# Attention's reciprocal sums go through the maxima's transpose and DRAM instead of four transposes a pair of heads

## The chip, the cores and the metric

The kernel runs on one core of a Trainium2 chip. The metric is the device time of one execution in microseconds (us); 2429.42 us is the median of three runs before the change (2428.42 to 2429.88). The engines named here are PE (TensorE, with PEld for its weight loads), DVE (VectorE), ACT (ScalarE), POOL (GpSimd) and SP, whose queue issues nearly all DMAs. Each engine works through its own queue in order.

## What is computed

The reference is one trunk layer over 2048 positions of 1024 channels: an RMS norm, one projection `W_in`, a spatial-gating group A, an attention group B, `W_out`, then a convolutional FFN and a last norm. The change lies in group B, eight heads of 64 channels:

```python
s = einsum('bhtd,bshd->bhts', qi, k) * scale
s = s + ci[..., :, None] - c[:, :, None, :]      # c: cumulated log-sigmoid of the forget logits
s = where(kpos[None, :] <= qpos[:, None], s, -inf)
p = softmax(s, axis=-1)
return einsum('bhts,bshd->bthd', p, v)
```

The softmax needs for each query the maximum of its scores and the sum of the exponentials; the output of a head is divided by that sum.

## The kernel before

All matmuls of the projections run with operands split into a high and a low float32r part (`mm3`, lines 208 to 212: three matmuls for one product). Phase A computes the projections of two halves of the sequence, phase C the output projection, phase D the FFN's up-projection, and a last phase the down-projection.

Attention is a stream (`b_stream`) of 32 pieces: four blocks of 512 queries (tb = 0 to 3), and in each eight heads. It is a Python generator that the big matmul loops advance: `tick` counts their matmuls, and for every 3.5 to 4.4 of them (`RATES`) the stream makes one step, so that its instructions are laid between those of the projections. A `yield` ends a step. The instructions so traced are then ordered, engine by engine, by a planner that gives each instruction a priority by its place in the program and times it with its own cost figures; the order in each queue is fixed at compile time.

A head has two parts:

- `b_max(h, tb)` loads the queries (`t1`, `t2`) and keys, computes the scores with queries on partitions (lines 750 and 751), takes their minima on DVE (754, 756; the sign is turned), exponentials with sums on ACT (759), and at its end the maxima `m8` (767, 768) and, by way of `lw` and `l1`, the reciprocal `rr` of the sum (773 to 778, for the first block 780): four numbers for each of 128 partitions, for the 4 x 128 queries.
- `b_mix(h, tb, ...)` computes the scores again with keys on partitions (811, 812), with the maxima as rows 96 to 104 of the stationary query tile `t1`, then the exponentials (817), their split (822, 823) and the product with the values into `po` (799, 800).

Between them stands `turn`: PE transposes `m8` (128x8, line 784) into a bank of the score ring, and DVE multiplies it by a selection mask `rowsel` into `t1` (785). The order of the work is `b_max(h+1)`, then `b_mix(h)`, which runs the `turn` of head h+1 at its step `TURN` = 3, then `b_max(h+2)`.

At the end of `b_mix` the two heads of a pair have written the halves of the partitions of `op` (834, 835). After the odd head the reciprocals of both heads are needed along the free axis, the same for 64 partitions of a head: ACT widens `rr` to `rw`, 128x512 (840); after a step, `transpose4` makes four PE transposes of 128x128 (line 183) into one bank of the score ring; and DVE multiplies `op` by it from PSUM (843). The result is split (196, 197) and stored to `mixh` and `mixl` in DRAM, from where the output projection reads it.

The score ring has three PSUM banks, with two more of another pool in the later part (`scores`). `op` and `rw` have one buffer each.

Of the kernel before, what the change touches and what calls it, by code (L numbers as in the profile page):

```python
# [80 lines left out]
class Block:  # L81
# [134 lines left out]
    def constants(self):  # L216
        nc, a, tc = self.nc, self.a, self.tc
        cp = self.cpool = self.ctx.enter_context(tc.tile_pool(name="const", bufs=1))
        self.ident = cp.tile([P, P], F32, name="ident")
        make_identity(nc, self.ident)  # L220
        self.mhalf = cp.tile([P, 8], F32, name="mhalf")
        nc.gpsimd.memset(self.mhalf, -0.5)
        self.cols = cp.tile([P, 200], F32, name="cols")
        self.halo = cp.tile([P, 2 * NF, 2], F32, name="halo")
        nc.gpsimd.memset(self.halo, 0.0)
        dp = self.ctx.enter_context(tc.tile_pool(name="dram", bufs=1, space=DRAM))
        self.ones_d = dp.tile([2, HALF], F32, name="ones_d")
        t = lambda n, k, s: [dp.tile(s, F32, name=f"{n}{i}") for i in range(k)]
        self.qx = t("qx", 2, [8, 128, HALF])
        self.kx = t("kx", 2, [8, 132, HALF])  # L230
        self.cc = t("cc", 2, [8, 2, HALF])
        self.vd = t("vd", 2, [HALF, 8, P])
        self.mixh = t("mixh", 4, [D, TB])
        self.mixl = t("mixl", 4, [D, TB])
        self.rows_d = [t(f"rows{i}_", 8, [P, D]) for i in range(2)]
        self.act_d = [t(f"act{i}_", NF, [P, HALF]) for i in range(2)]
        self.tw_d = t("tw", NF // 2, [P, 2, D])

    def columns(self):

# [409 lines left out]
    def b_consts(self):  # L650
        nc, bp = self.nc, self.bp
        ones = self.til(self.sp, [P, TB], F32, "st")[:2, :]
        nc.gpsimd.memset(ones, 1.0)
        for i in range(2):
            self.dma(self.ones_d[:, i * TB:(i + 1) * TB], ones)
        for k in self.kx:
            self.dma(k[:, 128:130, :], self.ones_d.unsqueeze(0).broadcast_to([8, 2, HALF]))
        self.mask = bp.tile([P, TB], BF16, name="mask")
        nc.gpsimd.memset(self.mask, 0.0)

        nc.gpsimd.affine_select(out=self.mask, in_=self.mask, compare_op=ALU.is_ge, fill=BIG, base=384,
                                pattern=[[-1, TB]], channel_multiplier=1)

        self.maskT = bp.tile([P, P], BF16, name="maskT")
        nc.gpsimd.memset(self.maskT, 0.0)
        nc.gpsimd.affine_select(out=self.maskT, in_=self.maskT, compare_op=ALU.is_ge, fill=BIG, base=0,
                                pattern=[[1, P]], channel_multiplier=-1)

        self.rowsel = bp.tile([8, 4, P], BF16, name="rowsel")
        nc.gpsimd.memset(self.rowsel, 1.0)  # L670
        for base, mult in ((0, 1), (1, -1)):
            nc.gpsimd.affine_select(out=self.rowsel, in_=self.rowsel, compare_op=ALU.is_ge, fill=0.0, base=base,
                                    pattern=[[-2 * mult, 4], [0, P]], channel_multiplier=mult)
        self.M1, self.T1 = [[self.til(self.mp, [P, TB], F32R, tag) for _ in range(2)] for tag in ("m1", "t1")]
        for m in self.M1:
            nc.gpsimd.memset(f32(m[64:128, :]), 0.0)
            nc.gpsimd.memset(f32(m[96:104, :]), 1.0)
        for t in self.T1:
            nc.gpsimd.memset(f32(t[64:128, :]), 0.0)
            self.dma(f32(t[66:68, :]), self.ones_d[:, 0:TB])  # L680

    def b_stream(self, pieces):

        todo = None
        for h, tb in pieces:
            if tb >= 2 and not self.ready:
                if todo:
                    yield from self.b_mix(*todo, None)
                    self.done += 1
                    todo = None  # L690
                while not self.ready:
                    yield
            t1, t2, turn = yield from self.b_max(h, tb)
            if todo:
                yield from self.b_mix(*todo, turn)
                self.done += 1
            else:
                turn()
            todo = (h, tb, t1, t2, self.rr)
        yield from self.b_mix(*todo, None)  # L700
        self.done += 1

# [27 lines left out]
    def b_max(self, h, tb):  # L730
# [8 lines left out]
        self.dma(f32(t2), self.qx[hf][h, :, sl])  # L739
        nm = self.til(bp, [P, 4, 4], F32, "part")  # L740
        ls = self.til(bp, [P, 4, 4], F32, "ls")
        if h % 2 == 0:
            self.rr = self.til(bp, [P, 4, 2], F32, "rr")
        for sb in range(tb + 1):
            m1, m2 = self.b_keys(h, sb, False)
            for tt in range(4):
# [16 lines left out]
            nc.vector.tensor_reduce(mx, nm[:, :, 0:tb + 1], axis=AX.X, op=ALU.min)  # L763
        else:
            nc.vector.tensor_copy(mx, nm[:, :, 0])
        m8 = self.til(bp, [P, 4, 2], F32R, "m8")
        nc.vector.tensor_scalar(m8[:, :, 0], mx, -1.0, None, ALU.mult)
        nc.vector.scalar_tensor_tensor(m8[:, :, 1], mx, -1.0, f32(m8[:, :, 0]), op0=ALU.mult, op1=ALU.subtract)
        rr = self.rr[:, :, h % 2]
        if tb:  # L770
            k = slice(0, tb + 1)
            lw = self.til(bp, [P, 4, 4], F32, "lw")
# [7 lines left out]
            nc.vector.reciprocal(rr, ls[:, :, 0])  # L780

        def turn():
            pm = self.scores([8, P])
            nc.tensor.transpose(pm, f32(m8).rearrange("p a b -> p (a b)"), self.ident)
            nc.vector.tensor_tensor(t1[96:104, :].rearrange("p (a b) -> p a b", a=4),
                                    pm.unsqueeze(1).broadcast_to([8, 4, P]), self.rowsel, op=ALU.mult)

        return t1, t2, turn

    def b_mix(self, h, tb, t1, t2, rr, turn):  # L790

        nc, bp, pp = self.nc, self.bp, self.bpp
        po = self.til(pp, [P, TB], F32, "o")
        ns = 4 * tb + 4
        late = []

        def pv():
            sc, c, v, ph, pl = late.pop(0)
            nc.tensor.matmul(po[:, c], lhsT=v, rhs=ph[:, c], start=sc == 0, stop=False)  # L799
            nc.tensor.matmul(po[:, c], lhsT=v, rhs=pl[:, c], start=False, stop=sc == ns - 1)  # L800

        for sc in range(ns):
            if sc == TURN and turn:
                turn()
            if sc % 4 == 0:
                m1, m2, v4 = self.b_keys(h, sc // 4, True)
            j = max(0, sc - 4 * tb)
            c = slice(j * P, TB)
            ks = slice((sc % 4) * P, (sc % 4 + 1) * P)
            ps = self.scores([P, TB])  # L810
            nc.tensor.matmul(ps[:, c], lhsT=m1[:, ks], rhs=t1[:, c], start=True, stop=False)  # L811
            nc.tensor.matmul(ps[:, c], lhsT=m2[:, ks], rhs=t2[:, c], start=False, stop=True)  # L812
            if sc >= 4 * tb:
                d = ps[:, j * P:(j + 1) * P]
                nc.vector.tensor_tensor(d, d, self.maskT, op=ALU.add)  # L815
            e = self.room([P, TB], F32, "e")
            nc.scalar.activation(e[:, c], ps[:, c], AF.Exp, scale=-1.0)  # L817
            if len(late) >= (LAG + 1 if self.more else LAG):
                pv()
            ph = self.room([P, TB], F32R, "ph")  # L820
            pl = self.room([P, TB], F32R, "pl")
            nc.scalar.activation(ph[:, c], e[:, c], AF.Copy)  # L822
            nc.vector.tensor_tensor(pl[:, c], e[:, c], f32(ph[:, c]), op=ALU.subtract)  # L823
            late.append((sc, c, v4[:, sc % 4, :], ph, pl))
            yield
        while late:
            pv()
            yield

        if h % 2 == 0:  # L830
            self.op = self.til(self.mp, [P, TB], F32, "op")
        op = self.op
        own, other = (slice(0, 64), slice(64, 128)) if h % 2 == 0 else (slice(64, 128), slice(0, 64))
        nc.scalar.activation(op[own, :], po[other, :], AF.Copy)
        nc.vector.tensor_tensor(op[own, :], po[own, :], op[own, :], op=ALU.add)
        if h % 2 == 0:
            return

        rw = self.til(self.mp, [P, 4, 2, 64], F32, "rw")
        nc.scalar.activation(rw, rr.unsqueeze(3).broadcast_to([P, 4, 2, 64]), AF.Copy)  # L840
        yield
        pr = self.transpose4(None, "s", [rw[:, i, :, :].rearrange("p a b -> p (a b)") for i in range(4)])
        nc.vector.tensor_tensor(op, pr, op, op=ALU.mult)
        oh = self.room([P, TB], F32R, "ph")
        ol = self.room([P, TB], F32R, "pl")
        self.split_sb(op, oh, ol)
        cs = slice(512 + (h - 1) * 64, 512 + (h + 1) * 64)
        self.dma(self.mixh[tb][cs, :], f32(oh))
        self.dma(self.mixl[tb][cs, :], f32(ol))
# [666 lines left out]
```

## Time and profile before

| | |
|---|---|
| median of the runs | 2429.42 us (2428.42 to 2429.88) |
| profiled execution | 2425.31 us, of which the span from first to last instruction 2423.6 us |
| granted TensorE clock, mean | 0.999 |
| PE / DVE / ACT / POOL busy | 2404.0 / 1755.0 / 1352.4 / 315.8 us |
| DMA | 400.51 MB, mean 165 GB/s |
| pairs of heads, transposes of `rw` on PE | 16, 64 |
| attention's first and last multiply by the reciprocals (843) | starts at 192.7 and 1491.2 us |

A line of a group reads: line, engine, operation, tiles out<-in, sizes, count, then busy us and mean ns of one, then idle time of the engine before it and what ended it. A line of a timeline reads: start in us from the span's start, duration in us, engine, line, operation, tiles, sizes, count, and in brackets the idle time before it with what ended it. Matmuls overlap, so their durations don't add up. L100 is the helper that issues DMAs, L183 the one that makes four transposes.

### The profile page before, as it was taken

The page shows a single profiled execution, that of the slowest core. Times are in us where ns is not written, and L with a number is a line of the kernel's source. Part 1 is how long each engine was busy: PE and PEld are TensorE (multiplying, and loading weights), DVE is VectorE, ACT ScalarE, POOL GpSimd, SP SyncE. Part 2 cuts the span into 40 slices and gives each one's busy share as a digit, 9 for nine tenths or more (in the row PEclk, how much of TensorE's full clock was granted, in tenths as well). Part 3 has the DMA queues.
Part 4 walks back from the last instruction along what each step waited for, and adds up shares of the span by engine and source line. Part 5 has one row for each costly group of instructions (what it writes and reads, how often), then busy time and mean ns, then how long its engine had stood idle before and what let it go on. Part 6 is the DMA issues. An engine that isn't in the chain of part 4 may idle for free.

```text
span 2423.6 us, 32604 instructions
## 1 busy us (share of the span) xinstructions
PE 2404.0 (99%) x10984; PEld 1981.1 (82%) x10984; DVE 1755.0 (72%) x3086; ACT 1352.4 (56%) x2635; POOL 315.8 (13%) x303
## 2 busy tenths in 40 slices
PE   9999999999999999999999999999999999999998
PEld 7788888788788888888888888888888888888887
DVE  5448785565568778878778775598888877957776
ACT  4347766554446555766776764365555455454443
POOL 3114140000241221111012101100000000000000
PEclk9999999999999999999999999999999999999999
DMA  8854636658855444555445565312222238538633
GB/s 291 276 142 120 202 114 178 170 169 265 261 188 183 160 163 161 163 170 181 149 154 180 165 190 199 130 52 88 86 79 87 85 95 306 164 99 296 207 118 122
DMA packets 245031, 400.51 MB, mean 165 GB/s; under 512 B 51240, under 2 KB 109736, under 8 KB 243440
## 3 DMA queue, kind: packets, MB, share of 16 engines
q1 hardware_dynamic: 239824, 374.31, 48.7%
q0 software_dynamic: 5040, 24.12, 2.6%
q8 instruction: 87, 1.43, 0.2%
q14 instruction: 80, 0.66, 0.1%
HBM read 304.76 MB, written 93.72 MB: 164 GB/s over the span
## 4 chain that ended last, share of the span: by engine, by line
PE 68%; DMA 2%; DVE 2%; ACT 1%; issue 1%; POOL 0%; SPq 0%; DVEq 0%; POOLq 0%; ACTq 0%
PE D L1356 14%; PE mm L212 8%; PE mm L208 8%; PE mm L210 8%; PE A L1154 3%; PE A L1156 3%; PE A L1155 3%; PE o L800 2%; PE o L799 2%; PE B L1156 2%; PE B L1155 2%; PE B L1154 2%; PE s L751 1%; PE s L750 1%; PE s L812 1%; PE s L811 1%
## 5 line engine op out<-in xcount | busy, mean ns | idle before, releaser
L210 PE MATMUL mm<-tlo,whi 128*128 128x512 f32 x912 | 358.3, 393 | 0.0
L212 PE MATMUL mm<-thi,wlo 128*128 128x512 f32 x912 | 357.5, 392 | 0.0
L208 PE MATMUL mm<-thi,whi 128*128 128x512 f32 x912 | 357.2, 392 | 0.0
L150 POOL TENSOR_SCALAR whi<-raw 128x1024 fp32r<-128x1024 f32 (+1 forms) x112 | 128.2, 1146 | 980.5 <-PE mm L210 576.5
L208 PE MATMUL mm<-whi,thi 128*128 128x512 f32 x640 | 252.0, 395 | 0.7 <-POOL whi L150 0.7
L212 PE MATMUL mm<-whi,tlo 128*128 128x512 f32 x640 | 251.5, 394 | 1.1 <-DMA tlo<-mixl 1.1
L210 PE MATMUL mm<-wlo,thi 128*128 128x512 f32 x640 | 251.1, 393 | 0.2
L759 ACT ACTIVATE s<-s,part 128x512 f32<-128x512 f32 (+3 forms) x261 | 154.6, 592 | 141.8 <-DVE part L754 85.2
L823 DVE TENSOR_TENSOR pl<-e,ph 128x512 fp32r<-128x512 f32 (+1 forms) x218 | 146.6, 681 | 76.0 <-ACT ph L822 42.4
L208 PEld LDWEIGHTS mm<-thi,whi 128*128 128x128 f32 x912 | 171.4, 188 | 35.9
L212 PEld LDWEIGHTS mm<-thi,wlo 128*128 128x128 f32 x912 | 171.5, 188 | 34.9
L210 PEld LDWEIGHTS mm<-tlo,whi 128*128 128x128 f32 x912 | 171.5, 188 | 34.9
L817 ACT ACTIVATE e<-s 128x512 f32<-128x512 f32 (+1 forms) x222 | 113.8, 529 | 109.5 <-DVE s L815 49.5
L162 DVE TENSOR_TENSOR wlo<-raw,whi 128x1024 fp32r<-128x1024 f32 x104 | 135.6, 1304 | 51.0 <-POOL whi L150 50.8
L822 ACT ACTIVATE ph<-e 128x512 fp32r<-128x512 f32 (+1 forms) x218 | 120.1, 563 | 43.6 <-PE o L799 41.1
L1356 PE MATMUL D<-wl,xh 128*128 128x512 f32 x368 | 141.4, 389 | 0.0
L1356 PE MATMUL D<-wh,xh 128*128 128x512 f32 x368 | 140.8, 389 | 0.2 <-DVE xo L1434 0.2
L212 PEld LDWEIGHTS mm<-whi,tlo 128*128 128x128 f32 x640 | 120.3, 188 | 24.7 <-DMA tlo<-mixl 1.4
L208 PEld LDWEIGHTS mm<-whi,thi 128*128 128x128 f32 x640 | 120.3, 188 | 24.3 <-POOL whi L150 1.0
L210 PEld LDWEIGHTS mm<-wlo,thi 128*128 128x128 f32 x640 | 120.3, 188 | 24.1 <-DVE wlo L162 1.0
L1356 PE MATMUL D<-wh,xl 128*128 128x512 f32 x368 | 137.2, 389 | 0.0
L754 DVE TENSOR_REDUCE part<-s 128x1 f32<-128x512 f32 x149 | 98.5, 683 | 26.6 <-PE s L751 25.9
(1860 smaller groups left out, 5834.8 us busy)
## 6 DMA issues: line engine op xcount, KB each, us to landing
raw<-in_w_up_dram SPq DMA_DIRECT2D x72, 512.0 KB
m<-kx SPq DMA_DIRECT2D x134, 256.0 KB
m<-kx SPq DMA_DIRECT2D x160, 136.0 KB
x<-act SPq DMA_DIRECT2D x84, 256.0 KB
raw<-in_w_in_dram SPq DMA_DIRECT2D x36, 512.0 KB
v<-vd SPq DMA_DIRECT2D x67, 256.0 KB
raw<-in_w_out_dram SPq DMA_DIRECT2D x24, 512.0 KB
tw<-in_w_down_dram SPq DMA_DIRECT2D x11, 1024.0 KB
```

The costliest lines, as they stand in the source:

```text
L150: self.cast_ins = self.nc.gpsimd.tensor_scalar(out, in_, 1.0, 0.0, ALU.mult, ALU.add).ins
L162: nc.vector.tensor_tensor(lo, raw, f32(hi), op=ALU.subtract)
L208: mm(ps, lhsT=ah[k], rhs=bh[k], start=k == 0, stop=False)
L210: mm(ps, lhsT=ah[k], rhs=bl[k], start=False, stop=False)
L212: self.last_mm = mm(ps, lhsT=al[k], rhs=bh[k], start=False, stop=k == n - 1).ins
L759: nc.scalar.activation(ps[:, :n], ps[:, :n], AF.Exp, scale=-1.0, bias=dst, accum_out=ls[:, tt, sb:sb + 1])
L822: nc.scalar.activation(ph[:, c], e[:, c], AF.Copy)
L823: nc.vector.tensor_tensor(pl[:, c], e[:, c], f32(ph[:, c]), op=ALU.subtract)
L1154: mm(ps, lhsT=xh[:, ks], rhs=yh[:, k, :], start=fresh and k == 0, stop=False, **kw)
L1155: mm(ps, lhsT=xh[:, ks], rhs=yl[:, k, :], start=False, stop=False, **kw)
L1156: mm(ps, lhsT=xl[:, ks], rhs=yh[:, k, :], start=False, stop=k == 3, **kw)
L1356: nc.tensor.matmul(bank[t], lhsT=x[i][:, ts], rhs=w[k], start=fresh and j == 0 and i + k == 0, stop=last and i == 1, **kw)
```

## The change

The reciprocals are written beside the maxima, into columns 8 to 11 of one tile of 12 columns, `m12`. The `turn` transposes the whole tile, 128x12. DVE takes rows 0 to 7 as before; ACT copies all twelve rows into one of three places on partitions 32, 64 and 96 of the tile whose first partitions hold `rowsel`, and SP stores rows 8 to 11, the reciprocals, four rows of 512 bytes, to a DRAM tensor `rl` of its pair. At the start of an odd head's `b_mix`, two DMAs load the 2 KB of each head of the pair to 64 partitions each, into the buffer that `rw` had. At the end DVE multiplies `op` by it from SBUF. The widening on ACT, the step after it, the four transposes and the tile `rr` are gone.

```diff
+        self.rl_d = t("rl", 16, [2, 4, P])
...
-        self.rowsel = bp.tile([8, 4, P], BF16, name="rowsel")
+        sel = bp.tile([P, 4, P], BF16, name="rowsel")
+        self.rowsel = sel[0:8]
+        self.turned_rows = [sel[i:i + 12].rearrange("p a b -> p (a b)")[:, 0:256].bitcast(F32) for i in (32, 64, 96)]
...
-        m8 = self.til(bp, [P, 4, 2], F32R, "m8")
+        m12 = self.til(bp, [P, 12], F32R, "m8")
+        m8 = m12[:, 0:8].rearrange("p (a b) -> p a b", b=2)
...
-        rr = self.rr[:, :, h % 2]
+        rr = f32(m12[:, 8:12])
...
         def turn():
-            pm = self.scores([8, P])
-            nc.tensor.transpose(pm, f32(m8).rearrange("p a b -> p (a b)"), self.ident)
+            pm = self.scores([12, P])
+            nc.tensor.transpose(pm, f32(m12), self.ident)
             nc.vector.tensor_tensor(t1[96:104, :].rearrange("p (a b) -> p a b", a=4),
-                                    pm.unsqueeze(1).broadcast_to([8, 4, P]), self.rowsel, op=ALU.mult)
+                                    pm[0:8, :].unsqueeze(1).broadcast_to([8, 4, P]), self.rowsel, op=ALU.mult)
+            self.turned_rows.append(self.turned_rows.pop(0))
+            pc = self.turned_rows[0]
+            nc.scalar.activation(pc, pm, AF.Copy)
+            self.dma(self.rl_d[4 * tb + h // 2][h % 2], pc[8:12, :])
...
+        if h % 2:
+            rl = self.til(self.mp, [P, 4, P], F32, "rw")
+            for i in range(2):
+                self.dma(rl[64 * i:64 * i + 64, :, :], self.rl_d[4 * tb + h // 2][i:i + 1, :, :].broadcast_to([64, 4, P]))
...
-        rw = self.til(self.mp, [P, 4, 2, 64], F32, "rw")
-        nc.scalar.activation(rw, rr.unsqueeze(3).broadcast_to([P, 4, 2, 64]), AF.Copy)
-        yield
-        pr = self.transpose4(None, "s", [rw[:, i, :, :].rearrange("p a b -> p (a b)") for i in range(4)])
-        nc.vector.tensor_tensor(op, pr, op, op=ALU.mult)
+        nc.vector.tensor_tensor(op, rl.rearrange("p a b -> p (a b)"), op, op=ALU.mult)
```

More of the change, by code (lines that the diff above doesn't have):

```diff
@@ L698, in b_stream @@
                 turn()
-            todo = (h, tb, t1, t2, self.rr)
+            todo = (h, tb, t1, t2)
         yield from self.b_mix(*todo, None)
@@ L741, in b_max @@
         ls = self.til(bp, [P, 4, 4], F32, "ls")
-        if h % 2 == 0:
-            self.rr = self.til(bp, [P, 4, 2], F32, "rr")
         for sb in range(tb + 1):
@@ L782, in turn, with b_mix @@
         def turn():
-            pm = self.scores([8, P])
-            nc.tensor.transpose(pm, f32(m8).rearrange("p a b -> p (a b)"), self.ident)
+            pm = self.scores([12, P])
+            nc.tensor.transpose(pm, f32(m12), self.ident)
             nc.vector.tensor_tensor(t1[96:104, :].rearrange("p (a b) -> p a b", a=4),
-                                    pm.unsqueeze(1).broadcast_to([8, 4, P]), self.rowsel, op=ALU.mult)
+                                    pm[0:8, :].unsqueeze(1).broadcast_to([8, 4, P]), self.rowsel, op=ALU.mult)
[3 more added lines that the diff above has]
+            self.dma(self.rl_d[4 * tb + h // 2][h % 2], pc[8:12, :])
         return t1, t2, turn
-    def b_mix(self, h, tb, t1, t2, rr, turn):
+    def b_mix(self, h, tb, t1, t2, turn):
         nc, bp, pp = self.nc, self.bp, self.bpp
```

## The prediction

> **What bounds the kernel now.** I read the page first: engine shares, then the chain that ended last.
>
> ```profile
> span 2423.6 us, 32604 instructions
> ...
> PE 2404.0 (99%) x10984; PEld 1981.1 (82%) x10984; DVE 1755.0 (72%) x3086; ACT 1352.4 (56%) x2635; POOL 315.8 (13%) x303
> ...
> PE 68%; DMA 2%; DVE 2%; ACT 1%; issue 1%; POOL 0%; SPq 0%; DVEq 0%; POOLq 0%; ACTq 0%
> ```
>
> TensorE is the only engine with something to do all the time. A share of the whole span says nothing about one stage, so the next view is the busy time by stretch, for the stretch from the end of the first pair of heads to the output of the last (188 to 1490 us):
>
> ```profile
> 188.00:1490.00 1302.00, 1297.39 (x6059) 1070.82 (x6058) 950.89 (x1876) 816.55 (x1730) 247.22 (x206) 1.00 0.57 177
> ```
>
> The columns are the length, then busy us of PE, PEld, DVE, ACT and POOL, the granted clock, the share and GB/s of the DMA engines. PE is idle for 1302.00 - 1297.39 = 4.6 us; DVE is at 73%, ACT at 63%, the clock at 1.00. So in this stretch an instruction taken from PE's queue shortens the time by what it holds up its successors, as long as no new wait fills the hole; and 4.6 us is all that smoother feeding could add.
>
> **The change part by part.**
>
> *Four transposes a pair leave PE.* There are 60 + 4 = 64 in 16 pairs, L183 reading rw:
>
> ```profile
> L183 PE MATMUL s<-ident,rw x60: 270/272/299, 188.2 to 1479.8; 128*128 128x128 f32 x60
> ...
> L183 PE MATMUL dn<-ident,rw x4: 270/272/275, 1289.0 to 1289.6; 128*128 128x128 f32 x4
> ```
>
> 272 ns is the time from start to end, and matmuls overlap; the price is what the queue moves back. The timeline of PE at the pair whose four stand together:
>
> ```profile
> 787.00 0.39 PE L799 MATMUL o<-ph,v 128*128 128x512 f32 x1
> 787.22 0.39 PE L212 MATMUL mm<-thi,wlo 128*128 128x512 f32 x1
> 787.46 0.60 PE L183 MATMUL s<-ident,rw 128*128 128x128 f32 x4
> 787.81 0.48 PE L208 MATMUL mm<-thi,whi 128*128 128x512 f32 x1
> 788.12 0.40 PE L210 MATMUL mm<-tlo,whi 128*128 128x512 f32 x1
> 788.36 0.40 PE L800 MATMUL o<-pl,v 128*128 128x512 f32 x1
> ```
>
> A 512-column matmul starts 0.22 to 0.24 us after the one before it. From 787.22 to 788.36 are 1.14 us with three of them (L212, L208, L210): 1.14 - 3 x 0.23 = 0.45 us for the four transposes. 16 pairs x 0.45 = **7.2 us off**.
>
> The Trainium skill, "TensorE: Matmul & The Clock Gate", Part 4: PE-mode transpose, gives about 275 ns for one 128x128 transpose in a kernel's context. The rows agree with that as a duration (272 ns) and not as a step in a filled queue (0.45/4 = 0.11 us); taken as the price it would give an estimate of 64 x 0.275 = 17.6 us, the third rival below.
>
> *The maxima's transpose gets 12 columns for 8.* Only the weight load grows:
>
> ```profile
> L784 PEld LDWEIGHTS s<-ident,m x30: 83/84/89, 143.8 to 1431.6; 128*8 128x8 f32 x30
> ...
> L784 PEld LDWEIGHTS dn<-ident,m x2: 84/84/84, 1174.5 to 1329.4; 128*8 128x8 f32 x2
> ```
>
> Even if its 84 ns grew in proportion (x 12/8, 42 ns) and nothing covered it, 32 x 0.042 = 1.3 us; but the loads overlap the matmuls before them (PEld is a row of its own in the page's first part), so I take 0.1, ends 0 and 1.3.
>
> *ACT and DVE.* Gone: 16 widenings L840. New: 32 copies of 12x128 from PSUM; the trace has none, so I bound it by a 128x16 activation below and a 128x128 exponential from PSUM above. The multiply L843 reads SBUF where it read PSUM; nearest is L197, both operands in SBUF.
>
> ```profile
> L840 ACT ACTIVATE rw<-rr 128x512 f32<-128x512 f32 x16 | 10.1, 632 | 2.9 <-DVE rr L778 2.5 <-DVE rr L780 0.3
> L817 ACT ACTIVATE e<-s 128x128 f32<-128x128 f32 x20 | 5.5, 274 | 20.5 <-DVE s L815 16.9 <-DVE pl L823 3.4
> L774 ACT ACTIVATE lw<-lw 128x16 f32<-128x16 f32 x8 | 1.8, 225 | 0.1
> ```
>
> ```profile
> L843 DVE TENSOR_TENSOR op<-s,op 128x512 f32<-128x512 f32 x15 | 10.3, 688 | 0.3
> L197 DVE TENSOR_TENSOR pl<-op,ph 128x512 fp32r<-128x512 f32 x12 | 8.4, 704 | 2.2 <-ACT ph L196 2.2
> ```
>
> ACT: 32 x 0.225 to 0.274 = 7.2 to 8.8 us for 10.1. DVE: 688 against 704 ns. Both engines have 350 us and more of idle time in the stretch that covers this; without that cover ACT's part would still be a gain of 1 to 3 us. I cost it at 0. One PSUM bank of the score ring is also freed for a while, which the four transposes held until L843 had read them; what that can give PE is part of the 4.6 us above, and I cost it at 0.
>
> *The turn now waits for the reciprocals.* This is the added wait on the path. L784 needed the maxima alone; now it needs L778's reciprocals too, which come five operations on DVE and ACT later. PE works its queue in order: if the reciprocals are late, every matmul behind L784 (the projections, the up-projections, the other head's scores) waits with it. So I compared the two in time. In four of the 32 heads the reciprocal ended after L784 had begun:
>
> ```profile
> 404.41 0.27 PE L784 MATMUL s<-ident,m 128*8 128x128 f32 x1
> ...
> 941.50 0.27 PE L784 MATMUL s<-ident,m 128*8 128x128 f32 x1
> ...
> 1074.25 0.27 PE L784 MATMUL s<-ident,m 128*8 128x128 f32 x1
> ...
> 1174.76 0.27 PE L784 MATMUL dn<-ident,m 128*8 128x128 f32 x1
> ```
>
> ```profile
> 405.53 0.17 DVE L778 RECIPROCAL rr<-l 128x4 f32<-128x4 f32 x1
> ...
> 941.54 0.18 DVE L778 RECIPROCAL rr<-l 128x4 f32<-128x4 f32 x1
> ...
> 1076.07 0.17 DVE L778 RECIPROCAL rr<-l 128x4 f32<-128x4 f32 x1
> ...
> 1174.87 0.17 DVE L778 RECIPROCAL rr<-l 128x4 f32<-128x4 f32 x1
> ```
>
> Late by 1.29, 0.22, 1.99 and 0.29 us: 3.8 us of stall if nothing were reordered, and some 0.2 us a time for the hand-over makes 4.6. But the planner knows of the new dependency and puts L784 behind the reciprocal as it times them, with other matmuls ahead; what is left is where DVE runs later than planned. Ends 0 and 4.6; I take **1.0 us**, nearer the low end because all waits of PE in this stretch together, for 6059 matmuls, are 4.6 us now.
>
> *32 stores and 32 loads on SP.* Per head ACT's copy is stored (2 KB); per odd head two loads fill 64 partitions each (128 KB). The multiply needs them late: the odd head of the first pair turns at 157.41, its product comes at 192.69, 35 us for a store and a load.
>
> ```profile
> 157.41 0.27 PE L784 MATMUL s<-ident,m 128*8 128x128 f32 x1
> ```
>
> ```profile
> 191.96 0.69 DVE L835 TENSOR_TENSOR op<-o,op 64x512 f32<-64x512 f32 x1
> 192.69 0.69 DVE L843 TENSOR_TENSOR op<-s,op 128x512 f32<-128x512 f32 x1
> ```
>
> L843 follows the addition L835 at once (191.96 + 0.69 = 192.65), so today's transposes don't delay it either: the pair's output comes neither earlier nor later. What counts is SP's queue, which is in order. A store stands there until ACT has copied, a load until its store has landed, and behind them stand the next head's queries, for which PE does wait now and then:
>
> ```profile
> 335.17 0.45 SPq L100 DMA_DIRECT2D t<-qx  x1
> 335.66 0.44 SPq L100 DMA_DIRECT2D t<-cc  x1
> 336.20 1.37 SPq L100 DMA_DIRECT2D t<-qx  x1
> ```
>
> ```profile
> 341.06 0.47 PE L750 MATMUL s<-m,t 96*128 96x512 f32 x1 [0.60 <-DMA t<-qx]
> ```
>
> A load's bytes, 256 KB a pair, take 256/177 = 1.4 us at the stretch's mean rate, if all of it fell ahead of the queries. Ends: 0, and 16 x 1.4 = 22 us when it does so at every pair. I take **0.5 us**: from the second block of queries on, the store is four or more steps of the mixing ahead of the queries' loads, and only the first block's heads have it close.
>
> Sum: -7.2 + 0.1 + 1.0 + 0.5 = **-5.6 us**. The profiled execution took 2425.3 us (span 2423.6 and 1.7 around it), which makes 2419.7. The runs' median, 2429.42, lies 4.1 above that execution; I carry the difference over: 2429.4 - 5.6 = **2423.8 us**, 0.23% less. 0.2%, or 4.9 us, is about what a measurement of this kernel can tell from no change.
>
> **The rivals.**
>
> 1. *The turn stalls PE in place of the transposes.* For it: four late reciprocals, on a DVE that is 73% busy and works in order. Against: the planner moves L784. Price 4.6 and more: -7.2 + 0.1 + 4.6 + 0.5 = -2.0, so 2427.4 (no change).
> 2. *SP's queue: loads of the reciprocals stand ahead of the queries.* PE waits at the first L750 of a head. The place is the end of each even head's mixing; the price up to 1.4 us at each of 16 pairs, and it decides from 0.45 us a pair on, where 16 x 0.45 eats the gain. At the full price: -7.2 + 0.1 + 1.0 + 22 = +16; at half, +5: 2434 to 2445 (**slower**). Against it: the queries' loads need t1's release at the end of the mixing, later than the store. The Trainium skill, "DMA: Bandwidth & Descriptors", Anatomy of one DMA, says that a semaphore is waited for on the issuing sequencer, and that about 2 us of a DMA are fixed cost, mostly the receipt of the write; no row here isolates that cost, and the estimate by it is 2 us for each load that is queued close behind its store.
> 3. *A transpose costs its duration.* 64 x 0.272 = 17.4 us off: 2412. Against it is the timeline above.
> 4. *The new order loses elsewhere what this place gives.* With 64 instructions fewer, another rotation of banks and one step less a pair, the planner lays everything from 188 us on anew; the 4.6 us of waits can double as well as shrink. Doubled it is 2423.8 + 4.6 = 2428.4 (no change); shrunk by 3, 2420.8.
> 5. *The gain isn't seen*: PE's time is not what the end follows. The 99% speak against it. 2429.
>
> **How the numbers follow.** Forecast (2421.5 to 2424.5) 0.49; rival 1, 0.19; rival 2, 0.10; rival 3, 0.02; rival 4 at no change 0.11 and with shrunk waits 0.07; rival 5, 0.02. Faster by over 0.2%: 0.49 + 0.02 + 0.07 = 0.58. Within: 0.19 + 0.11 + 0.02 = 0.32. Slower: 0.10. The range leaves out rival 3, most of rival 2 and the outer part of rival 4: 2418.5 to 2431. The likeliest case alone: 2421 to 2425.
>
> **What would show it right or wrong.** Right: PE's instructions 64 fewer; its busy time of the stretch 7 us less; its idle time still below 6 us; L784 behind L778 in all heads with gaps below 1 us. Rival 1 shows as waits of PE's L784 for the reciprocals; rival 2 as PE's L750 waiting for t from qx, with SP standing at a store or load of rl just before; rival 4 as waits on other lines. If PE's idle time is unchanged and the time falls by less than 5 us, the price of the transposes was wrong.

## The result and the profile after

The changed kernel takes 2434.71 us (median of nine runs, 2431.39 to 2439.78) against 2429.42 (nine runs, 2427.0 to 2432.07): a ratio of **1.0026, 95% interval 1.0016 to 1.0036**, slower by 5.3 us in the medians and 6.3 by the ratio, where 5.6 us less had been forecast. Its profiled execution took 2434.71 us, the span 2433.0.

The page of the changed kernel, engine shares and the chain that ended last:

```profile
span 2433.0 us, 32590 instructions
...
PE 2401.4 (99%) x10920; PEld 1974.8 (81%) x10920; DVE 1752.2 (72%) x3086; ACT 1350.4 (56%) x2651; POOL 314.6 (13%) x303
...
PE 85%; DMA 7%; DVE 4%; ACT 2%; issue 1%; POOL 1%; SPq 0%; DVEq 0%; POOLq 0%; ACTq 0%
```

PE has the 64 instructions less (10984 - 10920), and the chain has 7% of DMA where it had 2%. The same stretch as before, 188 to 1490 us, columns as in the prediction:

```profile
188.00:1490.00 1302.00, 1287.72 (x5968) 1059.37 (x5967) 946.10 (x1874) 815.89 (x1746) 245.77 (x206) 1.00 0.58 180
```

PE's idle time went from 4.6 to 14.3 us. In the same 1302 us it did 6059 - 5968 = 91 matmuls less, of which 64 are the missing transposes; the other 27, at 0.23 us, are the 6 us that it is behind. What it waited for is in the view of PE's waits (us in total, times, longest):

```profile
PE s L821 <- DMA m<-kx: 3.2, 2, 1.6
PE s L751 <- DMA m<-kx: 2.7, 3, 1.4
...
PE s L822 <- DMA m<-kx: 1.2, 2, 1.0
PE dn L821 <- DMA m<-kx: 1.2, 2, 0.8
```

8.3 us of waits for the keys, tile m loaded from kx, in nine stops. In the view of before no row of PE waits for m. Line 821 is what 811 was.

How a key load comes late is seen in SP's timeline of the changed kernel, and PE's a little later:

```profile
1444.07 0.33 SPq L100 DMA_DIRECT2D m2+_3147_13348<-kx  x1
1445.00 0.26 SPq L100 DMA_DIRECT2D rl<-rowsel  x1
1449.96 0.45 SPq L100 DMA_DIRECT2D rw<-rl  x1
1450.50 0.54 SPq L100 DMA_DIRECT2D raw<-in_w_out_dram  x1
1451.13 0.69 SPq L100 DMA_DIRECT2D m<-kx  x2
1452.65 0.37 SPq L100 DMA_DIRECT2D v<-vd  x1
1453.12 1.49 SPq L100 DMA_DIRECT2D m<-kx  x2
```

```profile
1455.24 0.39 PE L208 MATMUL mm<-thi,whi 128*128 128x512 f32 x1
1457.21 0.47 PE L821 MATMUL s<-t,m 128*128 128x512 f32 x1 [1.58 <-DMA m<-kx]
```

The store of the reciprocals is issued at 1445.00; the load that reads them stands at the head of SP's queue until 1449.96, 4.6 us, for the store to land; the weights and the keys stand behind it, and PE stops for 1.58 us. Over the whole run SP's own waits for the three things that the change put into its queue (ACT's copy, the landing of the store, the release of the buffer by the multiply L849) are:

```profile
SPq L100 <- ACT rowsel L791: 73.7, 24, 10.9
...
SPq L100 <- DMA rl<-rowsel: 41.3, 14, 4.6
...
SPq L100 <- DVE op L849: 23.5, 8, 5.8
```

### The profile page after: what moved, and what is told of

It reads as the page before. It is cut to its first block, busy times and chain, and to the rows that moved or that the text cites. A ratio compares the mean times of both kernels' runs of the same rounds, so it can differ in the third digit from the quotient of the medians.

```text
span 2433.0 us, 32590 instructions
## 1 busy us (share of the span) xinstructions
PE 2401.4 (99%) x10920; PEld 1974.8 (81%) x10920; DVE 1752.2 (72%) x3086; ACT 1350.4 (56%) x2651; POOL 314.6 (13%) x303
## 4 chain that ended last, share of the span: by engine, by line
PE 85%; DMA 7%; DVE 4%; ACT 2%; issue 1%; POOL 1%; SPq 0%; DVEq 0%; POOLq 0%; ACTq 0%
PE D L1362 15%; PE mm L210 12%; PE mm L208 12%; PE mm L212 12%; PE A L1160 3%; PE A L1161 3%; PE A L1162 3%; DMA m<-kx 3%; PE o L806 2%; PE o L805 2%; PE s L822 2%; PE s L821 2%; PE s L752 2%; PE s L751 2%; PE B L1161 2%; PE B L1162 2%
## 5 line engine op out<-in xcount | busy, mean ns | idle before, releaser
L833 DVE TENSOR_TENSOR pl<-e,ph 128x512 fp32r<-128x512 f32 (+1 forms) x219 | 141.4, 653 | 82.5 <-PE o L806 44.4
L210 PEld LDWEIGHTS mm<-wlo,thi 128*128 128x128 f32 x640 | 120.4, 188 | 23.5
```

Of the source, the lines that this page charges most:

```text
L210: mm(ps, lhsT=ah[k], rhs=bl[k], start=False, stop=False)
```

## The experiments

Every ratio is to the kernel before, run on the same chip beside it; the intervals are about 0.0009 to either side, 2 us, unless given. Two questions were asked: what the change costs beyond the gain, and where the gain of 7 us went. The expectations name five theories. Q: DMAs that stand in SP's queue hold up the loads behind them. P: each new order that the planner makes is a draw, with better or worse waits. S: what feeds PE (the other engines and the DMAs) is so close behind it that time saved on PE comes back as waits. B: the bytes of the new loads cost. R: the new turn costs. P can be tested directly, since the traces show the order of PE's queue: two runs can be compared matmul by matmul.

**The change without its DMAs.** The edit takes out the store and the loads and multiplies by ones:

```diff
-            self.dma(self.rl_d[4 * tb + h // 2][h % 2], pc[8:12, :])
...
-            rl = self.til(self.mp, [P, 4, P], F32, "rw")
-            for i in range(2):
-                self.dma(rl[64 * i:64 * i + 64, :, :], ...)
+            rl = self.rlc      # ones, set once
```

> The changed kernel without the stores and the loads of the reciprocals; op is multiplied by ones, so the division by the sums is left out of the output. The turn's 12 columns, ACT's copy and the missing four transposes stay. Theory Q (SP's queue: stores that wait for ACT's copy, loads that wait for their store to land, with the keys' loads behind them): the 7.2 us of the transposes come through, about 7 us below the kernel before, 2422, and PE's waits for m from kx (8.3 us in the changed kernel, none before) are gone. Theory P (the planner's new order by itself feeds PE worse): it stays about 5 us above the kernel before, 2434, with waits of PE of 10 us or more in the attention stretch. Theory B (the loads' 4 MB on the DMA engines): as Q.

2427.45 us, ratio 0.9994 (0.9985 to 1.0003). Neither 2422 nor 2434: the loss is gone, and the gain isn't there.

**Stores without loads**, the same with the store kept:

> The changed kernel with the stores but without the loads; op is multiplied by ones, the division is left out of the output. Theory Q: SP still stands for ACT's copy (73.7 us at 24 stores in the changed kernel) but no more for landings (41.3 us at 14 loads) or for the buffer (23.5 us at 8): some part of the loss stays, 2424 to 2430. Theory B: all of the gain, 2422. Theory P: 2434.

2425.97, ratio 0.9985 (0.9976 to 0.9993). The stores, for which SP stands longest, cost nothing. This run also speaks against a draw: 10843 of its 10920 matmuls stand at the same place of PE's queue as in the change, which is 0.0041, 10 us, slower and differs by the loads.

**Loads that wait for no store**, without the stores and from a tensor of ones:

```diff
-            self.dma(self.rl_d[4 * tb + h // 2][h % 2], pc[8:12, :])
...
-                self.dma(rl[64 * i:64 * i + 64, :, :], self.rl_d[4 * tb + h // 2][i:i + 1, :, :].broadcast_to([64, 4, P]))
+                self.dma(rl[64 * i:64 * i + 64, :, :], self.ones_d[i:i + 1, 0:TB].rearrange("o (a b) -> o a b", a=4).broadcast_to([64, 4, P]))
```

> The changed kernel without the stores; its loads have the same size and place (64 partitions, 2 KB each, two a pair) but read a tensor of ones that was written at the start, so they wait for no landing; the division is left out of the output. Theory B (bytes on the DMA engines): as the changed kernel, 2434, PE waits for m from kx. Theory Q: the loads no longer wait, and no store stands for ACT: 2422 to 2425. Theory P: 2434.

2430.32, ratio 1.0005 (0.9997 to 1.0014): 0.0011 above the run without DMAs, about 2.7 us, which is little more than the intervals; 0.0021, 5 us, below the whole change. All three theories missed: B and P said 2434, Q 2425 at most. The loads cost 2.7 us where there are no stores (e1 to e3) and 10 us where there are (e2 to the change), each time with PE's order from 960 us on nearly unchanged, so most of the loss needs the store that they wait for.

**The whole change with the loads moved** behind the last keys of the mixing:

```diff
-            for i in range(2):
-                self.dma(rl[64 * i:64 * i + 64, :, :], self.rl_d[4 * tb + h // 2][i:i + 1, :, :].broadcast_to([64, 4, P]))
...
+                if h % 2 and sc == ns - 4:
+                    with self.tc.issue_after(self.keys_ins):
+                        for i in range(2):
+                            self.dma(rl[64 * i:64 * i + 64, :, :], self.rl_d[4 * tb + h // 2][i:i + 1, :, :].broadcast_to([64, 4, P]))
```

> The changed kernel with the two loads of a pair put behind the last block of keys and values of the odd head's mixing on SP's queue, when the stores have long landed; the stores stay where they are. Theory Q: SP's waits for landings (41.3 us) and for the buffer (23.5 us) are gone and no load stands ahead of keys: near the run with stores and no loads, 2425 to 2428. Theory P: 2432 to 2436.

2427.34, ratio 0.9999 (0.9991 to 1.0008): 0.0027, 6.6 us, better than the change. PE's order is nearly that of the change (10301 of 10920 matmuls at the same place, and from 960 us on the two sequences agree in 99%), the bytes and the stores are the same, and the loads' place in SP's queue is what differs: here it is Q and neither P nor B. The pair was repeated at another order, with the stream's second rate 4.1 instead of 4.0 matmuls a step:

```diff
-RATES = [3.5, 4.0, 4.4, 3.6]
+RATES = [3.5, 4.1, 4.4, 3.6]
```

> The changed kernel with the stream's second rate 4.1 for 4.0: another order of the same work. The kernel before with 4.1 was at a ratio of 1.0008. If SP's queue is what costs the 5 to 6 us whatever the order (theory Q): again 4 to 6 us above the run with no transposes at the same rate, 2430 to 2435, with PE waiting for m from kx where a store or load of rl stands in front. If the loss was one bad draw of the order (theory P): 2425 to 2430 is as likely as 2435.

2435.50, ratio 1.0032 (1.0021 to 1.0043).

> The changed kernel with its loads behind the last keys of the odd head's mixing, and the second rate 4.1. The changed kernel at 4.1 was at a ratio of 1.0032. Theory Q (the loads stand in SP's queue for landings and for the buffer, with the keys behind them): the moved loads take 5 to 7 us off at this order too, 2427 to 2430, ratio 0.9995 to 1.0010. Theory P: 1.002 to 1.004 as well.

2425.32, ratio 0.9992 (0.9984 to 1.0001): 0.0040, nearly 10 us, better. At this rate PE's order from 960 us on differs between the two, so a part of the 10 us can be a draw. The place shows in the stretch from 960 to 1510 us (length, PE's busy time). The change at the two rates:

```profile
960.00:1510.00 550.00, 542.80 (x2438) 445.45 (x2438) 418.80 (x824) 361.43 (x807) 85.55 (x77) 1.00 0.54 171
```

```profile
960.00:1510.00 550.00, 542.13 (x2430) 443.31 (x2429) 416.04 (x821) 358.74 (x802) 85.26 (x77) 1.00 0.53 169
```

and with late loads at 4.0 and at 4.1:

```profile
960.00:1510.00 550.00, 547.20 (x2461) 449.71 (x2460) 420.05 (x826) 361.12 (x806) 88.42 (x79) 1.00 0.54 173
```

```profile
960.00:1510.00 550.00, 548.98 (x2470) 451.77 (x2469) 419.40 (x826) 362.21 (x804) 89.82 (x78) 1.00 0.55 173
```

PE is idle for 7.2 and 7.9 us with the loads as the change has them, for 2.8 and 1.0 with late loads. Of SP's waits with late loads at 4.0,

```profile
SPq L100 <- ACT rowsel L791: 64.2, 24, 10.8
...
SPq L100 <- DMA rl<-rowsel: 10.4, 4, 4.1
...
SPq L100 <- DVE op L851: 7.6, 3, 4.2
```

the landings fell from 41.3 to 10.4 us and the buffer's release from 23.5 to 7.6, while the waits for ACT's copy stayed (64.2 of 73.7). So it is the early loads in SP's queue that cost the change 6.6 us at its own order, and they cost it about as much or more at the other.

**The transposes alone.** The kernel before, without the widening, the step and the four transposes:

```diff
-        rw = self.til(self.mp, [P, 4, 2, 64], F32, "rw")
-        nc.scalar.activation(rw, rr.unsqueeze(3).broadcast_to([P, 4, 2, 64]), AF.Copy)
-        yield
-        pr = self.transpose4(None, "s", [rw[:, i, :, :].rearrange("p a b -> p (a b)") for i in range(4)])
-        nc.vector.tensor_tensor(op, pr, op, op=ALU.mult)
+        nc.vector.tensor_tensor(op, self.rlc.rearrange("p a b -> p (a b)"), op, op=ALU.mult)
```

> The kernel before with nothing changed but the widening, its step and the four transposes taken out; op is multiplied by ones, so the division by the sums is left out of the output; the turn has its 8 columns and waits for the maxima alone. Theory R (the new turn, with its wait for the reciprocals and ACT's copy, disturbs the feeding of PE even without a DMA): the 7.2 us come through, 2421 to 2422, and the four waits that the run without DMAs has at 303, 338, 348 and 358 us (4.4 us) are not there. Theory P (any order without the transposes is a new draw): 2425 to 2428, waits there or elsewhere.

2427.66, ratio 0.9998 (0.9989 to 1.0007). R falls: the old turn, and no gain. P's forecast, 2425 to 2428 with waits there or elsewhere, is what came. In its stretch from 188 to 1490 us PE is idle for 8.2 us, not 4.6:

```profile
188.00:1490.00 1302.00, 1293.77 (x5999) 1064.16 (x5998) 954.62 (x1879) 810.37 (x1716) 248.29 (x206) 1.00 0.56 177
```

6059 - 5999 = 60 matmuls less with 64 transposes gone: by 1490 us it is four matmuls, 0.9 us, ahead. Where the time goes back is the stretch from 290 to 365 us; before, and without the transposes:

```profile
290.00:365.00 75.00, 74.40 (x364) 62.21 (x363) 58.60 (x112) 53.96 (x98) 29.60 (x16) 1.00 0.45 129
```

```profile
290.00:365.00 75.00, 70.74 (x334) 57.16 (x333) 56.26 (x107) 53.63 (x93) 28.54 (x16) 1.00 0.37 112
```

0.6 us of idle time became 4.3. Two of the stops, from PE's timeline of the run without transposes:

```profile
338.09 0.93 PE L752 MATMUL s<-m,t 96*128 96x512 f32 x3 [1.74 <-DMA t<-qx]
...
348.06 0.50 PE L752 MATMUL s<-m,t 96*128 96x512 f32 x1 [1.50 <-ACT s L761]
```

and ACT's just before the second, first of the run without transposes, then two rows of the kernel before:

```profile
344.85 1.06 ACT L565 ACTIVATE vn<-ln 128x1024 f32<-128x1024 f32 x1 [4.67 <-DVE ln L562]
345.93 1.28 ACT L761 ACT_TABLE_LOAD   x1
347.23 0.66 ACT L761 ACTIVATE s<-s,part 128x512 f32<-128x512 f32 x1
```

```profile
341.40 1.06 ACT L565 ACTIVATE vn<-ln 128x1024 f32<-128x1024 f32 x1 [0.51 <-DVE ln L562]
...
346.37 0.66 ACT L759 ACTIVATE s<-s,part 128x512 f32<-128x512 f32 x1 [1.66 <-DVE part L754]
```

PE comes to the first scores at 338.09 where it came at 341.06, but ACT's first exponential on them starts at 347.23 where it started at 346.37: in front of it ACT waits 4.67 us for the layer norm on DVE (L562, which starts at 343.54 where it started at 340.16). PE fills the banks and stops. So PE is earlier here and what it waits for is later; the trace doesn't separate whether the stop comes of PE being early (S) or of the new order of the place (P). Other rates, 4.1 and 3.9, were run, each with a kernel of unchanged work beside it:

> The kernel before with the stream's second rate 4.1 matmuls a step for 4.0: the same work in another order. Theory P: off by several us, 2430 to 2436 most likely, with other waits of PE. If the order matters little: 2426 to 2430.

> The kernel before without the widening and the four transposes (op multiplied by ones, the division left out of the output), second rate 4.1. Theory P: a new draw, and with the rate changed the waits at 290 to 365 us need not come back: 2420 to 2426, on average 7 us under the kernel before at the same rate (1.0008). Theory S (what feeds PE is close behind it, so PE's saved time returns as waits): 2427 to 2430, waits of 3 us or more at 290 to 365 us or elsewhere in the attention stretch.

> The kernel before with the second rate 3.9 for 4.0: the spread of orders of the unchanged work. Theory P: 2426 to 2434. It is the base for the next run.

> The kernel before without the widening and the four transposes (the division left out of the output), second rate 3.9. Theory P: on average 7 us under the run before with 3.9. Theory S: the same as it within 2 us; with more steps per matmul the waits grow, 2428 to 2432.

| second rate | work as before | without the transposes | difference |
|---|---|---|---|
| 3.9 | 2428.68, 1.0002 | 2426.48, 0.9996 | -0.0006 |
| 4.0 | 1 | 2427.66, 0.9998 | -0.0002 |
| 4.1 | 2429.77, 1.0008 (0.9997 to 1.0019) | 2426.47, 1.0001 | -0.0007 |

On average -0.0005, 1.2 us, where 7.2 us are 0.0030; single differences are within the intervals. In the stretch from 290 to 365 us, without the transposes at 3.9 and at 4.1:

```profile
290.00:365.00 75.00, 70.27 (x333) 56.79 (x332) 56.27 (x106) 53.42 (x93) 28.65 (x16) 1.00 0.38 110
```

```profile
290.00:365.00 75.00, 70.69 (x336) 57.19 (x334) 57.23 (x109) 53.61 (x93) 28.59 (x16) 1.00 0.38 113
```

4.7 and 4.3 us again, against 0.5 and 1.1 with the transposes. But this is one order seen three times: the second rate sets in with the projections of the second half of the sequence, and the first matmul that stands elsewhere than at 4.0 comes at 595 us without the transposes (715 and 737 us with them). What the rates do show is how the loss lies in time. If the matmuls of two traces are lined up at equal work (each counted with the usual step of its shape, the transposes of `rw` with nothing), one can read how far one kernel is behind the other, in us, at the moment when the other stands at 188, 290, 365, 960 and 1490 us:

| | 188 | 290 | 365 | 960 | 1490 |
|---|---|---|---|---|---|
| without the transposes, 4.0 | 0.5 | -1.0 | 4.2 | 2.7 | -0.5 |
| the same at 3.9, against before at 3.9 | 0.3 | -1.1 | 4.7 | 1.4 | -1.2 |
| the same at 4.1, against before at 4.1 | 0.7 | -0.3 | 4.4 | 0.7 | -4.1 |
| the change | 2.7 | 2.3 | 7.0 | 3.6 | 8.3 |
| the change with late loads, 4.0 | 1.4 | 0.7 | 6.2 | 3.7 | 3.5 |

Without the transposes some 5 us are lost between 290 and 365 us, and from there to 1490 us 4.7, 5.9 and 8.5 us are gained, where twelve of the sixteen pairs are forecast to give 5.4. So the gain does come, and one place takes it back. (Runs with the same order up to 188 us differ there by 1.7 us, so a single figure is good to about that.) The change has the same loss at this place, and a second one, which late loads lack, from 960 us on. Whether every order without the transposes loses at this place is not shown: two of the runs below, f6 and g3, have another order here and only 1.2 and 0.6 us of idle time in this stretch, but by this count they too lose 3.7 and 3.3 us between 188 and 365 us.

**More transposes** instead of fewer:

```diff
         pr = self.transpose4(None, "s", [...])
+        for i in range(4):
+            nc.tensor.transpose(pr[:, i * P:(i + 1) * P], rw[:, i, :, :].rearrange("p a b -> p (a b)"), self.ident)
```

> The kernel before with eight transposes a pair instead of four, the second four writing the same again. If a transpose costs what it holds up in PE's queue (0.45 us for four): 16 x 0.45 = 7.2 us more, 2434 to 2435. If PE's time is slack that other engines and DMAs fill up to the same end (theory S, which would explain why taking four out gave nothing): 2427 to 2429. Theory P (each order is a new draw): anywhere from 2430 to 2440.

2441.37, ratio 1.0052 (1.0038 to 1.0067): 12.6 us for four more a pair, not 7.2, and above all three forecasts. The order is a new one here too, and some 5 us are its new waits, on top of what the transposes take.

**Parts of the change that turned out to cost nothing.** The step alone, out of the kernel before; then the turn with 12 columns and the wait for the reciprocals, without copy and DMAs:

> The kernel before without the step (yield) between the widening on ACT and the four transposes: the same instructions in another order from the first pair on. Theory P: moves by several us either way (more than 3 us off 2429), because each new order is a new draw of PE's waits. Theory Q: within 2 us of the kernel before.

2428.22, ratio 0.9996 (0.9987 to 1.0005). Its stretch from 290 to 365 us is idle for 0.3 us, so the missing step isn't what opens the hole there.

> The run without DMAs, and without ACT's copy: the turn has 12 columns and waits for the reciprocals, nothing reads rows 8 to 11; the division is left out of the output. If ACT's copy, which waits for DVE, is what costs: 2421 to 2422. If the wait of the turn for the reciprocals costs, or theory P holds: 2426 to 2428, as without DMAs.

2427.96, ratio 1.0000 (0.9991 to 1.0009), against 0.9998 with the old turn: the wait for the reciprocals costs nothing that can be measured.

**Stores on ACT's queue.**

```diff
-            self.dma(self.rl_d[4 * tb + h // 2][h % 2], pc[8:12, :])
+            nc.scalar.dma_start(self.rl_d[4 * tb + h // 2][h % 2], pc[8:12, :])
```

> The changed kernel with its 32 stores issued from ACT's queue, right behind the copy that they store, and the loads on SP as before. Theory Q: the 73.7 us that SP stood for ACT at 24 stores are gone; waits for landings stay: 2428 to 2432, and fewer waits of PE for m from kx than 8.3 us. Theory P: 2432 to 2436.

2429.63, ratio 1.0008 (0.9999 to 1.0017). Better than the change, by 0.0018, though SP stands longer for landings (58.1 us): the sum of SP's waits doesn't tell the loss, it matters which load stands behind them. But with the loads late as well it is worse than late loads alone, with and without the copy ahead of the multiplication:

> The changed kernel with stores on ACT's queue and loads behind the last keys, the copy behind DVE's multiplication as in the changed kernel. It is the run with three moves less the third, and the run with late loads plus the stores moved. Theory Q: 0.999 to 1.000, 2425 to 2428, and it is then the third move (the copy first) that cost 4 us in the run with all three. Theory P: anywhere from 1.000 to 1.003.

2431.38, ratio 1.0022 (1.0013 to 1.0030), within P's range and above Q's.

> The changed kernel with three things moved: stores on ACT's queue, loads behind the last keys of the odd head's mixing, and ACT's copy ahead of DVE's multiplication, so that it doesn't wait for it. Theory Q: all that SP lost by the change is back, as without DMAs, 2425 to 2427. Theory P: 2427 to 2434.

2432.15, ratio 1.0016 (1.0006 to 1.0026), the same. And with other rates:

> The run with the three moves, and the stream's first two rates 3.6 and 4.2 matmuls a step for 3.5 and 4.0, so that the waits at 303 to 358 us, where steps come sooner now than their loads, are planned anew. If these waits are a matter of the order alone (theory P): they go, 2420 to 2424. If PE has slack there (theory S): 2426 to 2428.

2438.92, ratio 1.0046 (1.0031 to 1.0060), 11 us and more above both forecasts. Q alone doesn't explain these three: SP waits less in them than in the change, and PE waits more elsewhere, for keys behind other loads, for ACT, for the output projection's inputs. PE's order is another one in each of them, so P fits, with 5.6 us between late loads with the store on SP (e8) and on ACT (e9). That is argued and not shown, and what in ACT's queue brings it is left open.

No kernel that does the whole work is clearly below the kernel before; late loads at 4.1 (0.9992, interval to 1.0001) come nearest.

## Why the prediction was wrong

**"An instruction taken from PE's queue shortens the time by what it holds up its successors"**, as long as no new wait fills the hole. This condition failed, and the sum had no term for it. The price in the queue was right: at the 16 pairs the four transposes, with the longer step of the matmul behind them, take 0.45 to 0.53 us beyond the usual steps, 7.7 us in all for a forecast of 7.2. But a hole did open: with the transposes alone gone some 5 us are lost between 290 and 365 us, and the runs gain 1.2 us on average. That PE was idle for only 4.6 of 1302 us said how well the old order fed it, and nothing of the new order, which is another one from the first pair on. It is rival 4, priced at up to 4.6 us and given 0.18 in both directions together. Why the new order has its hole at this place stays open.

**SP's queue, 0.5 us of a range from 0 to 22.** Mis-sized: the loads cost 10 us against the run without them, which has the same order of PE, and 6.6 of these come back when the loads stand late (0.0027; 0.0040 at another order). With the 3.6 us by which the run without loads is below the kernel before, all that the hole left of the 7.2, this makes the 6.3 measured. The mechanism was rival 2's, a load that stands in SP's queue for its store's landing; its victim and its place were wrong. I looked for late queries in the first block of queries, because there the store stands close to the queries' loads, and took the later blocks for safe since the product is 35 us and more away. But the loads don't stand where they are needed: at 1445 us the load follows its store in SP's queue and is waited for 4.6 us, for a product that comes at 1500.4, and what stood behind were keys. The 14 waits for landings come to 2.9 us each, where the prediction's estimate was 2 us for a load close behind its store. Four of the six stops for keys between 960 and 1510 us (at 1093, 1235, 1399 and 1455 us, together 4.2 us) have a load or a store of rl in front of the key load in SP's queue.

**The turn's wait for the reciprocals, 1.0 us.** It was 0. L786 starts 0.47 us or more behind the reciprocals in all 32 heads and PE never waits at it, as "the planner puts it behind" had it. The 3.8 us read off the four late heads didn't come; rival 1 is out.

**ACT, DVE and the 12 columns, 0.1.** Right. The load of 12 columns takes 86 ns for 84, the copy 267 ns, within the bounds of 225 and 274:

```profile
L786 PEld LDWEIGHTS s<-ident,m x28: 85/86/91, 145.7 to 1442.9; 128*12 128x12 f32 x28
```

```profile
L791 ACT ACTIVATE rowsel<-s 12x128 f32<-12x128 f32 x28 | 7.5, 267 | 12.1 <-DVE t L787 11.5
```

The last columns of the copy's row are something that was overlooked: ACT's copy waits for DVE's multiplication of the same bank, 11.5 us. It does no harm by itself: the run without DMAs, which has the copy, is at 0.9994.

**The profiled execution of before**, 2425.3 us, lay below all nine runs (2427.0 at least). Carrying its distance over to the runs was right; comparing the two profiled executions (9.4 us) would have overstated the loss.

Rivals 2 and 4 happened together, and each was priced alone: a new order that loses 5 us at one place, and a queue that loses 10. The time lies just inside rival 2's 2434 to 2445 us, but that is luck: this figure held the full gain of 7.2 us against 11 us or more of waits for queries. Rival 5 is out: the gain is seen in PE's steps.

## What to carry to other kernels

An engine that is 99% busy under one order needn't be so under the next: taking work out of its queue makes a new order, whose waits the old profile doesn't show. Take the work out by itself before building what replaces it: here four transposes less were worth 1.2 us, four more cost 12.6. Then line up the two traces at equal work to see where the gain went, and make sure that a variation meant as another order does change the order at the place in question: here the rates left it as it was. A DMA that reads what another DMA wrote held up all of SP's queue until the landing; put such a load behind the loads that the bounding engine waits for.

## What the runs showed of the hardware

A store of 2 KB from four partitions to DRAM held the load that reads it for 4.6 us in one place, and 14 loads for 41.3 us together, 2.9 us each; the queue stood behind them. A stop of PE costs a little more than the idle time that the trace puts against it: before the stop at 1457.21 the step from 1455.24 is 1.97 us, of which the usual 0.23 and the 1.58 marked leave 0.16. It is the overlap that is lost: the idle time is counted from the end of the matmul before, which lasted 0.39 us where the next usually starts after 0.23.
